# Row-wise dot products with running maximum and record count: one loop for all position groups, and tail masks made in pairs

## Chip, core and metric

The kernel runs on one core of a Trainium2 chip. The metric is the device time of one execution in microseconds; less is better.

## What is computed

```
B, S, D = 8, 2048, 4096            # x: (8, 2048, 4096), w: (4096, 1), float32
proj = (x @ w).squeeze(-1)         # (8, 2048): one dot product of 4096 for each row of x
cm = np.maximum.accumulate(proj, axis=1)
is_record = (proj >= cm).astype(np.float32)
return np.cumsum(is_record, axis=1)
```

For each batch and position: the dot product of a row of x with w, the running maximum over the positions, and a running count of the positions at which the maximum was reached. x is 268 MB and is read once; everything else is small.

## The kernel before

Rows of x lie in the 128 partitions, r of them side by side in each. Work is staged in four groups of positions, `RS = (4, 4, 4, 3)` rows per partition. A tile is one batch of one group: 128 partitions x r x 4096 numbers, 8 MB with four rows and 6 MB with three. Each group has eight tiles, batch 7 first. Then comes a tail: the last 128 positions, as eight tail tiles of 2 MB that hold four batches x 32 positions each, one row per partition; tail tiles 6 and 7 are cut into seven pieces by columns (`LAST`), so that little is left to do after the last one lands.

Three buffers (`xbuf`) hold the tiles. SP issues every load, in program order (L170 for the groups, L198 for the tail), and each load waits until the user before of its buffer is done: `free()` names the semaphore, `fr[t]`, which DVE and ACT each raise once, or `p7` for tile 7, which PE raises. In the first three groups tile t lies in buffer t mod 3, so tiles 6 and 7 lie in buffers 0 and 1, and tiles 0 and 1 of the group after take these again; in the fourth group `at` shifts the buffers by two. Tail tiles 0 to 2 lie in the quarter of the buffers which three-row tiles leave free, the others in the places of tiles 5 and 6.

A row is split by columns. DVE multiplies and sums the first 2816 columns in one instruction per row (`dot`, L126). POOL multiplies the last 1280 columns in place, one instruction per row (`tensor_mul`, L278), and ACT sums the products of each row (`add_up`, L132) as soon as POOL has raised `pl` for it. So each partition ends with two partial sums per row, `sum_v` and `sum_p`.

After a group's last tile PE (`group_rows`, L305 to L319) resets the semaphores and turns the partial sums into rows: two matmuls with the identity per row of the partition, which add `sum_p` and `sum_v` in PSUM (`ps`: 8 batches x 512 positions). DVE then runs `scans` (L140 to L150): running maximum, comparison, running count. Each engine has its own loop over the first three groups (`V.Fori`, `G.Fori`, `A.Fori`, `T.Fori`), and the fourth group's code stands after it in a straight line. DVE's loop begins with the scan of the group before; for the first group that is a scan of a constant (L248).

In the tail (L372 to L414) a tile's sums stand in partitions that mix batches and positions. Two constants sort them: `by_b` (partition to batch) and `by_i` (partition to position). For each tail tile POOL masks DVE's sum with `by_b` (`pick`, L349) and ACT masks its own (`pick_a`, L354); after every second tile PE multiplies the masks with `by_i` (`turn`, L359). DVE's scans of the fourth group stand behind tail tile 2 (384 positions), those of the tail behind tail tile 4 (64), behind piece 1 (32) and at the end (32). In each engine's queue the instructions stand in the order in which this Python code calls them.

Of the kernel before, what the change touches and what calls it, by code (L numbers as in the profile page):

```python
# [13 lines left out]
ALU = mybir.AluOpType  # L14
ACTF = mybir.ActivationFunctionType
NEG = -3.0e38
LOW = -3.2e38
# [3 lines left out]
def kernel(  # L21
# [16 lines left out]
    P = 128  # L38
# [3 lines left out]
    RS = (4, 4, 4, 3)  # L42
    R = RS[0]
    NS = 3
    NG = len(RS)
    NL = NG - 1
    N = R * P
    STARTS = [sum(RS[:g]) * P for g in range(NG)]
    S0 = sum(RS) * P
    assert S0 + P == S  # L50
# [5 lines left out]
    H = 4  # L56
    Q = P // H
# [9 lines left out]
    SEED = (None, 0, None, None, 2, 3, 4)  # L67
# [22 lines left out]
    masked = sb([P, 10 * B], "masked")  # L90
# [13 lines left out]
    sum_v, sum_p = cut(R * B), cut(R * B)  # L104
# [6 lines left out]
    def sem(name):  # L111
# [4 lines left out]
    ws, bw, wc, cs, od, oe, psr, pd, pl, sd, pa, con, fo, ms, p7, mg, pg, ml = (  # L116
        sem(n) for n in "ws bw wc cs od oe psr pd pl sd pa con fo ms p7 mg pg ml".split()
    )

    xq = [(ws, 32), (bw, NW + 16), (wc, 3 + 16), (con, 7 + 16), (fo, 1 + 16)]  # L120
    xq += [(s, 32) for s in xs[:5]] + [(s, 2 * NG + 16) for s in fr[:3]]
# [30 lines left out]
    def at(g, t):  # L152
        return xbuf[(t if g < NL else t + NS - 1) % NS]

    def user_before(g, t):
        if t >= NS:
            return t - NS, g + 1
        if g == NL:
            return B - NS + t, g
        return max(u for u in range(B) if u % NS == t), g  # L160
# [3 lines left out]

    with tc.tile_critical(no_gpsimd_drain=True):

        for g in range(NG):
            r = RS[g]
            for t in range(B):
                i = SY.dma_start(  # L170
                    out=at(g, t)[:, : r * D],
                    in_=x[B - 1 - t, STARTS[g] : STARTS[g] + r * P, :].rearrange(
                        "(p r) d -> p (r d)", r=r
                    ),
                ).then_inc(xs[t], 16)
                u, n = user_before(g, t)
                if n:
                    i._wait_ge(*(free(u, n)))
                if g == t == 0:
                    A.dma_start(  # L180
                        out=w_row, in_=w.rearrange("(k c) one -> k (c one)", k=NW)
                    ).then_inc(ws, 16)
                if t == 4 and g:
                    SY.dma_start(
                        out=out[:, STARTS[g - 1] : STARTS[g]], in_=cnt
                    )._wait_ge(cs, g + 1).then_inc(od, 16)

        def slot(m):
            if m < NS:
                return None, xbuf[m][:, RS[-1] * D :]  # L190
            u = B - NS if m < 2 * NS else B - NS + 1
            return u, at(NL, u)[:, (m % NS) * D : (m % NS + 1) * D]

        freed = {None}
# [23 lines left out]
        G.memset(cm[:, N - 1 :], NEG).then_inc(con, 1)  # L218
        G.memset(cnt[:, N - 1 :], 0.0).then_inc(con, 1)
# [3 lines left out]
        for n, k in enumerate(order):  # L223
# [15 lines left out]

        V.tensor_reduce(  # L240
            out=by_b, in_=identity.rearrange("p (i b) -> p b i", b=H),
            op=ALU.add, axis=mybir.AxisListType.X,
        )._wait_ge(con, 7)
        V.tensor_reduce(  # L244
            out=by_i, in_=identity.rearrange("p (i b) -> p i b", b=H), op=ALU.add,
            axis=mybir.AxisListType.X,
        ).then_inc(fo, 1)
        V.memset(ps[:B, :N], LOW)._wait_ge(wc, 3).then_inc(psr, 1)  # L248

        def group_scans(r=R):  # L250
            n = r * P
            scans(cm[:, :n], cnt[:, :n], ps[:B, :n], cm[:, N - 1 :], cnt[:, N - 1 :])

        def group_dots(r, g=0):
            for t in range(B):
                b, xb = B - 1 - t, at(g, t)
                for j in range(r):
                    i = dot(
                        xb[:, j * D : j * D + VC], w_v[:, :VC],
                        sum_v[:, j * B + b : j * B + b + 1],  # L260
                    )
                    if j == 0:
                        i._wait_ge(xs[t], 16)
                i.then_inc(fr[t], 1)

        with V.Fori(0, NL):
            group_scans()
            V.sem_inc(psr, -3)
            group_dots(R)
        group_scans()  # L270
        V.sem_inc(psr, -3)
        group_dots(RS[-1], NL)

        def group_products(r, g=0):
            for t in range(B):
                for j in range(r):
                    xl = at(g, t)[:, j * D + VC : (j + 1) * D]
                    i = G.tensor_mul(out=xl, in0=xl, in1=w_sb).then_inc(pl, 1)  # L278
                    if j == 0:
                        i._wait_ge(xs[t], 16)  # L280

        G.wait_ge(wc, 3)
        with G.Fori(0, NL):
            group_products(R)
            G.wait_ge(pg, 1).then_inc(pg, -1)
        group_products(RS[-1], NL)

        def group_sums(r, g=0):
            for t in range(B):
                b = B - 1 - t  # L290
                for j in range(r):
                    i = add_up(
                        at(g, t)[:, j * D + VC : (j + 1) * D],
                        sum_p[:, j * B + b : j * B + b + 1],
                    )._wait_ge(pl, j + 1)
                i.then_inc(fr[t], 1)
                A.sem_inc(pl, -r)
            A.wait_ge(pd, 1).then_inc(pd, -1)

        with A.Fori(0, NL):  # L300
            group_sums(R)
        group_sums(RS[-1], NL)

        def group_rows(r):
            T.wait_ge(fr[B - 1], 2).then_inc(p7, 1)  # L305
            T.sem_inc(fr[B - 1], -2)
            if r == R:
                for s in xs:
                    T.sem_inc(s, -16)
                T.sem_inc(pg, 1)  # L310
            T.wait_ge(od, 16).then_inc(od, -16)  # L311
            for j in range(r):
                for k, l in enumerate((sum_p, sum_v)):
                    i = T.matmul(  # L314
                        out=ps[:B, j : r * P : r], lhsT=l[:, j * B : (j + 1) * B],
                        rhs=identity, start=k == 0, stop=k == 1,
                    )
                    if j == r - 1:
                        i.then_inc((pd, psr)[k], 1)  # L319

        with T.Fori(0, NL):
            group_rows(R)
        group_rows(RS[-1])
# [34 lines left out]
        def turn(n, k, start, stop):  # L358
            return T.matmul(  # L359
                out=ps[:B, k * Q : (k + 1) * Q], lhsT=masked[:, n * B : (n + 1) * B],  # L360
                rhs=by_i, start=start, stop=stop,
            )

        def tail_scans(k0, k1, base):
            c = S0 - STARTS[-1]
            a, b = k0 * Q, k1 * Q
            scans(
                cm[:, c + a : c + b], cnt[:, c + a : c + b], ps[:B, a:b],
                cm[:, c + a - 1 : c + a], cnt[:, c + a - 1 : c + a], base,
            )  # L370

        for m in range(B - 2):  # L372
            k = m // 2
            v, p = acc_v[:, m : m + 1], acc_p[:, m : m + 1]
            sums(m, v, p)
            pick_a(col(2 * k, m), p)
            pick(G, col(2 * k + 1, m), v)._wait_ge(sd, nv).then_inc(mg, 1)
            if m == 2:
                group_scans(RS[-1])
            if m == 4:  # L380
                tail_scans(0, 2, 4)
            if m % 2:
                if k != 1:
                    T.wait_ge(cs, NG + 1 + k // 2)
                turn(2 * k, k, True, False)._wait_ge(ms, m + 1)
                mm = turn(2 * k + 1, k, False, True)._wait_ge(mg, m + 1)
                if k:
                    mm.then_inc(psr, 1)

        npart = [0, 0]  # L390
        for i in range(B - 2, len(TILES)):
# [8 lines left out]
            if p:  # L400
                pick_a(col(6 + npart[z], m), dp)
                npart[z] += 1
            if n in (1, len(LAST) - 2):
                pick(G, col(8, m), v)._wait_ge(sd, nv).then_inc(mg, 1)
            if n == 1:
                tail_scans(2, 3, 7)
        assert npart == [2, 2]
        pick(V, col(9, 1), v)._wait_ge(sd, nv).then_inc(ml, 1)
        T.wait_ge(cs, NG + 3)
        turn(6, 3, True, False)._wait_ge(ms, B - 2 + 3)  # L410
        turn(7, 3, False, False)._wait_ge(ms, B - 2 + 4)
        turn(8, 3, False, False)._wait_ge(mg, B)
        turn(9, 3, False, True)._wait_ge(ml, 1).then_inc(psr, 1)
        tail_scans(3, 4, 10)  # L414
        for a, b, n in ((STARTS[-1], S0, 1), (S0, S, 4)):
            SY.dma_start(
                out=out[:, a:b], in_=cnt[:, a - STARTS[-1] : b - STARTS[-1]]
            )._wait_ge(cs, NG + n).then_inc(oe, 16)
# [31 lines left out]
```

## Time and profile before

| | us |
|---|---|
| median of three runs (629.64, 630.08, 630.17) | 630.08 |
| the profiled execution | 629.62 |
| its span, first to last instruction | 627.84 |
| DVE busy | 407.2 |
| POOL busy | 370.5 |
| ACT busy | 181.1 |
| PE busy | 29.4 |

The difference between the profiled execution and its span, 1.78 us, lies around the span. In the lines of the profile, L126 is line 126 of the kernel; "a<-b" is the tile written and those read; "DVE xall L126" in a wait or a chain is what the waiting engine was released by. SPq and PEq are the instruction queues of SP and PE.

The order of one four-row tile in mid-run, from the timeline (start, duration): it lands and POOL starts at 139.52, four products to 151.01; ACT's first sum starts at 142.45 and its last read-out ends at 152.41; SP issues the next load into that buffer at 152.43. The next tile's products start at 158.82, 19.3 us after this one's.

### The profile page before, as it was taken

The numbers are of one execution on the slowest core, as the hardware profiler recorded it, in microseconds if no ns is written. First come the engines' busy times: TensorE is split into PE (matmuls) and PEld (weight loads), VectorE is DVE, ScalarE is ACT, GpSimd is POOL, SyncE is SP. The second block draws the span as 40 slices with busy tenths as digits, with TensorE's granted clock in tenths as the row PEclk, the third lists the DMA queues.
The fourth block names the chain that finished last, engine by engine and source line by source line (L and its number), as shares of the span: only waits on it lengthen the run. The fifth ranks groups of instructions, "written<-read, shape, count | busy, mean of one in ns | idle before, by whom it ended". The sixth has DMA issues, their size and how long they took to land. (4 is left out here: it accounts for less than half of the span.)

```text
span 627.8 us, 1141 instructions
## 1 busy us (share of the span) xinstructions
PE 29.4 (5%) x96; PEld 13.6 (2%) x96; DVE 407.2 (65%) x294; ACT 181.1 (29%) x274; POOL 370.5 (59%) x149
## 2 busy tenths in 40 slices
PE   8000000000020000000001000000002000000110
PEld 3000000000010000000000000000001000000000
DVE  0755676456776557755578655676556976655797
ACT  1222332123322233222233222332223333232244
POOL 0554676456765557745567555676557666655775
PEclk9999999999999999999996555555555555555565
DMA  9999999999999999999999999999999999999996
GB/s 402 401 468 401 468 401 464 406 463 405 463 405 463 405 463 405 465 405 463 405 463 405 463 405 459 409 460 409 459 420 423 436 442 420 443 442 410 430 429 261
DMA packets 6579, 268.55 MB, mean 428 GB/s; under 512 B 768, under 2 KB 1040, under 8 KB 1584
## 3 DMA queue, kind: packets, MB, share of 16 engines
q1 hardware_dynamic: 6560, 268.50, 98.9%
q14 instruction: 3, 0.02, 0.0%
q10 hardware_dynamic: 16, 0.02, 0.0%
HBM read 268.45 MB, written 0.07 MB: 428 GB/s over the span
## 5 line engine op out<-in xcount | busy, mean ns | idle before, releaser
L126 DVE CUSTOM_DVE_ANT_0 xall<-xall,w_v 128x2816 f32<-128x2816 f32 (+1 forms) x129 | 385.5, 3041 | 180.5 <-DMA xall<-in_x_dram 180.5
L278 POOL TENSOR_TENSOR xall<-xall,w_sb 128x1280 f32<-128x1280 f32 x120 | 344.8, 2905 | 245.9 <-DMA xall<-in_x_dram 242.6
L132 ACT ACTIVATE xall<-xall 128x1280 f32<-128x1280 f32 (+2 forms) x130 | 162.9, 1253 | 427.7 <-POOL xall L278 407.2
L314 PE MATMUL ps<-identity,small 128*8 128x128 f32 x60 | 13.4, 415 | 567.2 <-PEq L311 567.2
L132 ACT ACTIVATION_READ_ACCUMULATOR xall<-xall 128x1 f32 x130 | 24.2, 186 | 0.0
L338 POOL TENSOR_TENSOR xall<-xall,w_sb 128x1280 f32<-128x1280 f32 (+2 forms) x8 | 21.0, 2628 | 3.1 <-DMA xall<-in_x_dram 3.0
L314 PEld LDWEIGHTS ps<-identity,small 128*8 128x8 f32 x60 | 7.5, 128 | 574.3 <-issue 570.2
L142 DVE TENSOR_TENSOR_SCAN cm<-ps,cm,small 8x512 f32<-8x512 f32 (+3 forms) x8 | 7.0, 869 | 19.2 <-PE ps L314 18.8
L226 PE MATMUL w_v<-w,identity 8*128 8x512 f32 x14 | 12.2, 1056 | 0.0
L126 DVE DVE_READ_ACCUMULATOR2_ANT small<- 128x1 f32 x133 | 10.8, 81 | 0.0
L248 DVE MEMSET ps<- 8x512 f32 x1 | 0.5, 485 | 15.7 <-ACT w L237 15.7
L148 DVE TENSOR_TENSOR_SCAN cnt<-ps,cnt,small 8x512 f32<-8x512 f32 (+3 forms) x8 | 7.0, 871 | 0.3
L226 PEld LDWEIGHTS w_v<-w,identity 8*128 8x128 f32 x14 | 4.6, 332 | 7.3 <-issue 7.3
L234 ACT COPY w_sb<-w_v 128x768 f32<-128x768 f32 x1 | 0.8, 798 | 11.4 <-PE w_v L226 11.4
L145 DVE TENSOR_TENSOR ps<-ps,cm 8x512 f32<-8x512 f32 (+3 forms) x8 | 3.9, 486 | 0.3
L349 POOL TENSOR_TENSOR masked<-fold,small 128x4 f32<-128x4 f32 x8 | 1.6, 200 | 3.2 <-DVE small L126 3.2
L126 DVE CUSTOM_DVE_ANT_0 xall<-xall,w_v,small 128x480 f32<-128x480 f32 (+2 forms) x4 | 3.1, 810 | 0.2 <-DVE small L126 0.2
L359 PE MATMUL ps<-fold,masked 128*8 128x32 f32 x20 | 2.0, 234 | 25.3 <-ACT masked L354 17.7
L354 ACT ACTIVATE masked<-fold,small 128x4 f32<-128x4 f32 x10 | 3.0, 298 | 0.3
L338 POOL TENSOR_TENSOR xall<-xall,w 128x640 f32<-128x640 f32 (+1 forms) x2 | 2.3, 1136 | 0.1
L226 PE MATMUL ps<-w,identity 8*128 8x512 f32 x2 | 2.1, 1136 | 2.6 <-DMA w<-in_w_dram 2.6
L233 ACT ACT_TABLE_LOAD x1 | 1.3, 1283 | 2.7 <-DVE fold L244 2.7
(18 smaller groups left out, 5.3 us busy)
## 6 DMA issues: line engine op xcount, KB each, us to landing
xall<-in_x_dram SPq DMA_DIRECT2D x8, 6144.0 KB, 33.5
xall<-in_x_dram SPq DMA_DIRECT2D x6, 2048.0 KB, 42.6
xall<-in_x_dram SPq DMA_DIRECT2D x1, 1264.0 KB, 36.6
xall<-in_x_dram SPq DMA_DIRECT2D x1, 816.0 KB, 39.3
xall<-in_x_dram SPq DMA_DIRECT2D x1, 784.0 KB, 37.9
xall<-in_x_dram SPq DMA_DIRECT2D x2, 240.0 KB, 26.6
xall<-in_x_dram SPq DMA_DIRECT2D x1, 416.0 KB, 39.4
xall<-in_x_dram SPq DMA_DIRECT2D x24, 45.0
```

The costliest lines, as they stand in the source:

```text
L126: return V.tensor_tensor_reduce(out=xsl, in0=xsl, in1=wsl, scale=1.0, scalar=seed, op0=ALU.mult, op1=ALU.add, accum_out=dst,)
L132: return A.activation(out=xsl, in_=xsl, func=ACTF.Copy, accum_out=dst)
L142: V.tensor_tensor_scan(out=cm_, data0=src, data1=low, initial=cm0, op0=ALU.max, op1=ALU.max,)._wait_ge(psr, base).then_inc(psr, 1)
L145: V.tensor_tensor(out=src, in0=src, in1=cm_, op=ALU.is_ge)._wait_ge(psr, base + 1).then_inc(psr, 1)
L148: V.tensor_tensor_scan(out=cnt_, data0=src, data1=low, initial=cnt0, op0=ALU.add, op1=ALU.max,)._wait_ge(psr, base + 2).then_inc(cs, 1)
L226: i = T.matmul(out=dst, lhsT=identity[:NW, k : k + 1].to_broadcast([NW, P]), rhs=w_row, start=True, stop=True,).then_inc(bw, 1)
L278: i = G.tensor_mul(out=xl, in0=xl, in1=w_sb).then_inc(pl, 1)
L314: i = T.matmul(out=ps[:B, j : r * P : r], lhsT=l[:, j * B : (j + 1) * B], rhs=identity, start=k == 0, stop=k == 1,)
L338: G.tensor_mul(out=xl, in0=xl, in1=w_pool(*p))._wait_ge(*xq[i]).then_inc(pl, 1)
L349: return eng.tensor_tensor(out=e, in0=by_b, in1=acc.to_broadcast([P, H]), op=ALU.mult)
L354: return A.activation(out=e, in_=by_b, func=ACTF.Copy, scale=acc)._wait_ge(pa, na).then_inc(ms, 1)
L359: return T.matmul(out=ps[:B, k * Q : (k + 1) * Q], lhsT=masked[:, n * B : (n + 1) * B], rhs=by_i, start=start, stop=stop,)
```

## The change

All engines run one loop over four groups (`nc.Fori(0, NG)`). The first three are as before, eight tiles of 128 partitions x 4 rows. The fourth has six tiles of the same 8 MB, each of four batches x 128 positions: a partition holds four positions of one batch. Tiles 6 and 7, PE's matmuls and DVE's scan stand under an `If` that is false in the fourth round; the scan stands now behind the group's tiles. `at` is t mod 3 in all groups. The sixth tile is loaded in two halves, with a semaphore of its own for the second (`xh`).

POOL multiplies the four rows of a tile in one instruction, with w repeated for each; of the sixth tile two rows in each of two instructions. ACT waits once for it and then sums the four rows.

After the loop POOL adds `sum_v` and `sum_p` of the fourth group and masks them all in one instruction each (L355, L359), and PE makes the rows from them in 12 matmuls with `by_i`. In the tail, POOL waits after every second tile for DVE's and ACT's sums of both, adds them and masks them (L425, L429), and PE needs one matmul for a pair. The scan of the fourth group's 384 positions and that of the first 64 of the tail are one scan of 448 behind tail tile 4. Tail tiles 0 to 3 are loaded into the place of tile 3, the others into that of tile 4. The second piece of tail tile 6 no longer starts from the first one's sum; POOL masks both instead. The constants `by_i` are made by POOL. DVE's and ACT's programs are aligned (`addr_align`).

Instructions built: DVE 182 before and 129 now, ACT 117 and 83, POOL 113 and 76, PE 67 and 72, SP 68 and 74.

The diff, cut to what the text speaks of:

```diff
-    RS = (4, 4, 4, 3)
-    R = RS[0]
+    R = 4
     NS = 3
...
-    SEED = (None, 0, None, None, 2, 3, 4)
+    SEED = (None, None, None, None, 2, 3, 4)
...
-    def at(g, t):
-        return xbuf[(t if g < NL else t + NS - 1) % NS]
+    def at(t):
+        return xbuf[t % NS]
...
+                else:
+                    b0, s0 = (1 - t % 2) * H, STARTS[g] + t // 2 * P
+                    src = x[b0 : b0 + H, s0 : s0 + P, :].rearrange(
+                        "b (q r) d -> q b (r d)", r=R
+                    )
...
+                if g == NL and t == NT - 1:
+                    i = SY.dma_start(
+                        out=at(t)[:, :half], in_=src[:, :, :half]
+                    ).then_inc(xs[t], 16)
+                    SY.dma_start(
+                        out=at(t)[:, half:], in_=src[:, :, half:]
+                    ).then_inc(xh, 16)
...
         def slot(m):
-            if m < NS:
-                return None, xbuf[m][:, RS[-1] * D :]
-            u = B - NS if m < 2 * NS else B - NS + 1
-            return u, at(NL, u)[:, (m % NS) * D : (m % NS + 1) * D]
+            u = NT - NS + m // 4
+            return u, at(u)[:, m % 4 * D : (m % 4 + 1) * D]
...
-                for j in range(r):
-                    xl = at(g, t)[:, j * D + VC : (j + 1) * D]
-                    i = G.tensor_mul(out=xl, in0=xl, in1=w_sb).then_inc(pl, 1)
...
+        def products(t):
+            rows = at(t).rearrange("p (r d) -> p r d", r=R)
+            n = R // 2 if t == NT - 1 else R
+            for j in range(0, R, n):
+                xl = rows[:, j : j + n, VC:]
+                i = G.tensor_mul(
+                    out=xl, in0=xl, in1=w_one.to_broadcast([P, n, PC])
+                ).then_inc(pl, 1)
+                landed(i, t, j)
...
+        def row_sums(t):
+            for j in range(R):
+                c = COL(t, j)
+                i = add_up(at(t)[:, j * D + VC : (j + 1) * D], sum_p[:, c : c + 1])
+                if j == 0 or t == NT - 1 and j == R // 2:
+                    i._wait_ge(pl, 1)
...
+        with nc.Fori(0, NG) as g:
+            for t in range(NT):
+                dots(t)
+                products(t)
+                row_sums(t)
+            with nc.If(NL - g):
+                for t in range(NT, B):
+                    dots(t)
+                    products(t)
+                    row_sums(t)
+                G.wait_ge(pg, 1).then_inc(pg, -1)
+                A.wait_ge(pd, 1).then_inc(pd, -1)
+                group_rows()
+                scan_to(0, N, 1)
+                V.sem_inc(psr, -3)
...
         for m in range(B - 2):
             k = m // 2
             v, p = acc_v[:, m : m + 1], acc_p[:, m : m + 1]
             sums(m, v, p)
-            pick_a(col(2 * k, m), p)
-            pick(G, col(2 * k + 1, m), v)._wait_ge(sd, nv).then_inc(mg, 1)
-            if m == 2:
-                group_scans(RS[-1])
             if m == 4:
-                tail_scans(0, 2, 4)
+                scan_to(0, NE + 2 * Q, 1)
             if m % 2:
-                if k != 1:
-                    T.wait_ge(cs, NG + 1 + k // 2)
-                turn(2 * k, k, True, False)._wait_ge(ms, m + 1)
-                mm = turn(2 * k + 1, k, False, True)._wait_ge(mg, m + 1)
+                two = sum_t[:, 2 * k : 2 * k + 2]
+                G.wait_ge(sd, nv)
+                G.tensor_tensor(
+                    out=two, in0=acc_v[:, m - 1 : m + 1], in1=acc_p[:, m - 1 : m + 1],
+                    op=ALU.add,
+                )._wait_ge(pa, na).then_inc(mk, 1)
+                G.tensor_tensor(
+                    out=masked[:, k * B : (k + 1) * B].rearrange("p (z b) -> p z b", b=H),
+                    in0=two.rearrange("p (z o) -> p z o", o=1).to_broadcast([P, 2, H]),
+                    in1=by_b.rearrange("p (o b) -> p o b", o=1).to_broadcast([P, 2, H]),
+                    op=ALU.mult,
+                )._wait_ge(mk, 3 + k).then_inc(mg, 1)
+                if k == 2:
+                    T.wait_ge(cs, NL + 1)
+                mm = turn(k, k, True, True)._wait_ge(mg, k + 1)
...
-            if n in (1, len(LAST) - 2):
-                pick(G, col(8, m), v)._wait_ge(sd, nv).then_inc(mg, 1)
+            if n in (0, 1, len(LAST) - 2):
+                pick(G, col(5 + (n == 0), m), v)._wait_ge(sd, nv).then_inc(mg, 1)
             if n == 1:
-                tail_scans(2, 3, 7)
+                scan_to(NE + 2 * Q, NE + 3 * Q, 4)
```

## Prediction

> **What bounds the kernel now.** I read the page's head first, then the time slices, the queues, the waits of the DMA queue, and last the order of time at the end of the run.
>
> ```profile
> span 627.8 us, 1141 instructions
> DMA  9999999999999999999999999999999999999996
> q1 hardware_dynamic: 6560, 268.50, 98.9%
> ```
> The load queue holds all 16 DMA engines for 98.9% of the span: the stream of x is the bound, in every slice but the last.
>
> ```profile
> SPq L170 <- ACT xall L132: 414.2, 20, 38.9
> ```
> SP waits 414 us in all for ACT to free a buffer, yet the DMA engines never run dry: each load is issued while at least one whole tile is still moving. That wait is cover, and I ask below where it gets thin.
>
> ```profile
> 480.00:500.00 20.00, 3.57 (x16) 1.97 (x16) 13.66 (x12) 5.04 (x9) 11.59 (x5) 0.50 1.01 435
> 622.00:623.00 1.00, 0.00 (x0) 0.00 (x0) 1.00 (x5) 0.97 (x3) 0.73 (x1) 0.50 0.13 47
> 623.00:624.00 1.00, 0.28 (x3) 0.11 (x4) 1.00 (x4) 0.90 (x4) 0.20 (x1) 0.50 0.00 0
> ```
> (Last column GB/s.) 435 GB/s in mid-run; the last byte starts before 623. From there to the end, 627.84, nothing but the tail is left: about 4.9 us.
>
> ```profile
> 613.21 3.09 DVE L126 CUSTOM_DVE_ANT_0 xall<-xall,w_v 128x2816 f32<-128x2816 f32 x1 [0.89 <-DMA xall<-in_x_dram]
> 613.26 2.90 POOL L338 TENSOR_TENSOR xall<-xall,w_sb 128x1280 f32<-128x1280 f32 x1 [1.53 <-DMA xall<-in_x_dram]
> ...
> 616.39 0.20 POOL L349 TENSOR_TENSOR masked<-fold,small 128x4 f32<-128x4 f32 x1 [0.23 <-DVE small L126]
> 616.54 1.88 POOL L338 TENSOR_TENSOR xall<-xall,w_sb 128x800 f32<-128x800 f32 x1
> ...
> 620.19 1.75 POOL L338 TENSOR_TENSOR xall<-xall,w_sb 128x736 f32<-128x736 f32 x1
> ```
> Start, duration, and in brackets the idle time before. At tail tile 5 (613.2) both engines still waited for data, by 0.89 and 1.53 us: that is all the slack left there. After it they run almost back to back.
>
> ```profile
> 620.19 1.76 POOL xall L338
> 621.95 0.02 issue
> 621.97 0.92 ACT xall L132 x2
> 622.88 0.02 issue
> 622.91 0.30 ACT masked L354
> 623.21 0.41 ACT xall L132 x2
> 623.61 0.02 issue
> 623.64 0.31 ACT masked L354
> ```
> The chain that ended last: POOL's product of 736 columns, ACT's sum, mask, sum, mask (to 623.95), then PE and the last scans to 625.41, output to 627.84. DVE's own last mask ends at 624.24, so both end within 0.3 us of each other.
>
> [...] here 1280 elements take 2.90 us and 256 take 0.73, a slope of 2.12 ns plus 0.19 fixed[...]. [...] The trace shows three instruction packets, 0.0%, and no idle time of DVE, ACT or POOL put down to fetching, so shorter programs have nothing visible to win. [...]
>
> ```profile
> POOL masked L349 <- DVE small L126: 3.2, 5, 1.4
> ```
> POOL idles up to 1.4 us for a mask with its next product queued behind.
>
> **The change, part by part.** All in the profiled execution's frame (span 627.84, run 629.62); it lies 0.46 below the median, and I add the sum to the median.
>
> *Loads.* The same 268 MB. Packets of 64 KiB take 2.418 us and of 48 KiB 1.815 (the trace's packet records); per DMA engine 64 x 1.815 = 116.16 becomes 48 x 2.418 = 116.06: -0.1 us. The four-batch pattern is the tail's own (L198), which already moves 423 GB/s and more with rows of 16 KiB; I take no change. Tail landings thus move by -0.1.
>
> *One product of four rows, then four sums.* Before, a tile was free about 12.9 us after landing: tile 6 of the first group landed at 139.5 and SP issued the next load into its buffer at 152.43. Now POOL's 5120 elements take 0.19 + 5120 x 2.12 = 11.0 us (by slope) to 11.5 (four rows as now), and only then ACT sums four rows, each 1.27 + 0.19 overlapped to about 1.38: 5.5. Sum 16.6 to 17.1. Within a group three buffers rotate, and 19.3 us more cover it. At a group's end they do not: tiles 6 and 7 use buffers 0 and 1, and tiles 0 and 1 of the next group want these two again. Cover there is one tile: landing to the dry queue is 19.32 - 0.43 (last packet to landing) = 18.9 us for the slowest DMA engine and 18.3 for the others (the packet records show one 0.6 us behind); from issue to first packet takes 1.03 (0.97 to 2.00 at the start). 17.1 + 1.0 = 18.1. So it still fits, by 0.2 to 0.8 us. Cost taken: 0, three times. Without the cover, it costs 3 x the overrun.
>
> *Start.* DVE loses a memset and an empty first scan (18.29 to 22.11), POOL gains two small additions at 2 us; both end before the first tile lands (22.8). 0.
>
> *Scan at the loop's end.* DVE waits for PE there and then starts tile 0: about 5 + 3.2 us late, under a tile period of 19.3 against 12.3 of work; SP's output DMA waits behind tile 1's buffer anyway. 0. The same for branches, the nine semaphore steps on PE, and SP's empty loop, which runs after its last load is issued (about 603.6) and before its last store (625.4).
>
> *Last tile in halves, and its masks.* Its second half lands at about 583.9; POOL ends it at 589.7, ACT at 592.6. POOL waits for that (L355), then two small operations (0.45 together, from the 0.20 mask rows, bounds 0.3 to 0.8): first tail product at 593.35 against 592.69. The wait for data absorbs this: before tile 5 POOL is through at 611.9 by the same sum, and that tile lands at 613.1.
>
> *Pairs on POOL in the tail.* Removed: six ACT masks and six POOL masks. Added: after every second tile POOL waits for ACT's sum of the tile it has just multiplied, then adds, then masks. For tile 5: landing 613.1, product to 616.05, ACT (1.27 + 0.19 with its start) to 617.45, add and mask to 617.95. Before, POOL went on at 616.54. Behind it in its queue stand the products of the last two tiles: 800 columns 618.0 to 619.9, mask 0.2 (an added one), 640 columns to 621.7, mask to 621.9, 736 columns to 623.7. Before, that last one ended at 621.95. From there ACT's chain is unchanged, 2.0 us (621.95 to 623.95): 625.7. Three short matmuls wait for it, 0.5, then the scans from 626.25 against 624.61: **+1.65 us**. Price range: add and mask 0.3 to 0.8, so +1.5 to +2.0; if ACT's sum were somehow early, the DVE path below is left.
>
> *One scan of 448 in place of 384 and 64.* It stands after tile 4, no longer after 2. By size (384: 2.56 us, 64: 0.96) 448 takes 2.9. DVE: tile 4 to 611.3, scan to 614.2, tile 5 1.0 us late; then back to back 3.0, 1.88, 1.11, 0.72 (scan), 1.0, 0.94, 0.57, 0.64, 0.71, mask: 625.0 against 624.24: +0.75, beside POOL's path and under it.
>
> Sum +1.65: 631.3 in the profile's frame, **631.7** as median.
>
> **Rivals.** (a) Forecast, POOL's pair wait sets the end: 631.7. For it: the 1.53 us of slack is less than what is added. (b) POOL's small operations or ACT are quicker than taken and DVE's scan sets the end: 630.08 + 0.75 = 630.8; against it, 0.9 us would have to vanish. (c) Not slower: the shorter programs save around the span. Its place is the 1.78 us between run and span (629.62 - 627.84) and the 0.97 before the first load; a saving of 1.65 gives 630.1, and from 0.4 on the change can no longer be told from none. DVE goes from 182 to 129 instructions, ACT 117 to 83, POOL 113 to 76; against it stand the three packets[...]. (d) The two buffers at the group's end are late: if the four-row product with its repeated w takes 12.5 instead of 11.5, or the first packet comes later, 3 x 0.8 on top: 634. It decides from about 11.8 us per product. For it: the margin is the thinnest in the run. (e) Products in rows are far slower on POOL, past 19.3 us a tile: POOL becomes the bound, 30 x 23 = 690.
>
> **Chances.** (a) 0.62, (b) 0.14, (c) 0.08, (d) 0.14, (e) 0.02. A difference of 0.2%, 1.26 us, is about what measuring this kernel tells from none; that line is at 631.34. Slower by more: most of (a) (0.54), (d), (e): 0.70. Within: the rest of (a), (b), most of (c): 0.28. Faster: 0.02, as the stream alone ends at 622.9. Range 630.4 to 633.4: (a), (b) and the near part of (d), leaving out (c), the far part of (d) and (e).
>
> **What would show it.** POOL's first product of the last two tiles starts near 618 with no DMA wait before it; L425 shows about 1.4 us waits for ACT, three times; the chain that ends last goes POOL, ACT, PE, DVE, ending near 629.5. DMA 9 in all slices: a bubble at 157, 312 and 467 us, or a landing gap over 19.4, would be (d). Last x bytes at 622.8. I am wrong if the tail's POOL reaches the 736 product before 621, or the stream ends after 623.5.

## Result and profile after

| | before | changed |
|---|---|---|
| median, us (five runs each) | 629.78 | 636.84 |
| lowest to highest | 629.64 to 630.17 | 636.08 to 636.97 |
| span of the profiled execution | 627.8 | 634.7 |

The ratio is 1.0107, 95% interval [1.0092, 1.0121]: slower by 7.1 us, where 1.6 was forecast. The time lies above the stated range (630.4 to 633.4).

From the head of the changed kernel's page, and its load queue:

```profile
span 634.7 us, 1139 instructions
...
DMA  9999999999999999999999999999999999999994
...
q1 hardware_dynamic: 6416, 268.50, 98.4%
```

The row of nines says that nothing happened. A nine is any share of 90% or more in 15.9 us: a gap of 1 us is invisible there, and 98.4% instead of 98.9% is 3 us of all 16 engines in a longer span. The gap has to be looked for where the forecast's rival (d) put it, at the group ends. First POOL's order of time around the third of them (start, duration, in brackets the idle time before), for tiles 6 and 7 and tile 0 of the next group, in the changed kernel:

```profile
451.44 11.05 POOL L302 TENSOR_TENSOR xall<-xall,w_sb 128x5120 f32<-128x5120 f32 x1 [8.13 <-DMA xall<-in_x_dram]
470.76 11.04 POOL L302 TENSOR_TENSOR xall<-xall,w_sb 128x5120 f32<-128x5120 f32 x1 [8.26 <-DMA xall<-in_x_dram]
492.42 11.02 POOL L302 TENSOR_TENSOR xall<-xall,w_sb 128x5120 f32<-128x5120 f32 x1 [10.62 <-DMA xall<-in_x_dram]
```

POOL starts 0.07 us after a landing, so its starts show the landings: 19.32 us from tile 6 to 7, but 21.66 to tile 0. In the kernel before, tile 0 follows tile 7 by 19.32 us, as evenly as any other (the first group end):

```profile
158.82 11.49 POOL L278 TENSOR_TENSOR xall<-xall,w_sb 128x1280 f32<-128x1280 f32 x4 [7.81 <-DMA xall<-in_x_dram]
178.14 11.49 POOL L278 TENSOR_TENSOR xall<-xall,w_sb 128x1280 f32<-128x1280 f32 x4 [7.83 <-DMA xall<-in_x_dram]
```

At the changed kernel's third group end SP issues tile 0's load, into the buffer of tile 6, at 467.67:

```profile
467.67 0.63 SPq L194 DMA_DIRECT2D xall<-in_x_dram  x1
```

It comes 16.3 us after tile 6 landed and 3.0 us before tile 7 landed. The DMA engines around it (last two columns: busy share, GB/s by the start of packets):

```profile
466.00:468.00 2.00, 0.00 (x0) 0.00 (x0) 0.00 (x0) 1.65 (x4) 0.00 (x0) 0.50 0.76 328
468.00:469.00 1.00, 0.00 (x0) 0.00 (x0) 0.00 (x0) 0.00 (x0) 0.00 (x0) 0.50 0.01 0
469.00:470.00 1.00, 0.00 (x0) 0.00 (x0) 0.00 (x0) 0.00 (x0) 0.00 (x0) 0.50 3.07 983
```

Packets last 2.42 us and are counted where they start, so single columns swing. But two us at 328, one at 0 and one at 983 make 410 GB/s on average, where the kernel before moved 435 in mid-run, and by the packet records three packets are moving just before 469.07: 13 of the 16 engines are empty at once. Fifteen engines start their next packet 1.40 to 1.95 us after SP's issue. The sixteenth has data until 470.36 and starts its next packet at 471.69, 4.02 us after the issue. These first packets take 2.8 to 3.7 us instead of 2.42; at the kernel's start 14 of the 16 take 2.9 to 3.5. The tile's last packet ends on the sixteenth engine, at 492.00, and POOL starts at 492.42. That engine loses 1.33 us empty and 0.94 us in a packet of 3.36: nearly all of the 2.34 by which tile 0 is late.

"Slip" below is how much later tiles 0 and 1 landed together than two periods of 19.32 after tile 7. At the three group ends it is 0.85, 1.42 and 2.33 us: 4.6.

The end, in the chain that ended last:

```profile
618.36 2.91 POOL xall L390
621.30 1.37 ACT xall L134 x2
622.67 0.07 issue
622.74 0.20 POOL small L425
622.94 0.07 issue
623.01 0.20 POOL masked L429
623.21 1.83 POOL xall L390
625.04 0.16 POOL masked L401
625.21 1.49 POOL xall L390
626.70 0.16 POOL masked L401
626.86 1.71 POOL xall L390
628.59 0.92 ACT xall L134 x2
...
631.66 0.27 DVE cnt L150
```

The chain of the kernel before ended with:

```profile
625.14 0.27 DVE cnt L148
```

This is the forecast's tail, line by line: tail tile 5, ACT's sum, POOL's two small operations, then the products of the last two tiles with no wait for data before them. From the start of POOL's product of tail tile 5 to the end of the last scan it takes 13.57 us (618.36 to 631.93), before 12.15 (613.26 to 625.41): +1.42.

So of 6.9 us of span, tail tile 5 comes 5.1 late (618.36 against 613.26: 4.6 at the group ends, 0.26 at the first landing, 0.2 elsewhere), the tail adds 1.4, and the end after the last scan 0.3. The executions also spend more time around the span: 2.2 us instead of 1.8 (636.97 against a span of 634.7, 629.62 against 627.8). No run here shows what it is.

### The profile page after: what moved, and what is told of

Its sections match the earlier page's. It is cut to its first block, busy times and chain, and to the rows that moved or that the text cites. A ratio compares the mean times of both kernels' runs of the same rounds, so it can differ in the third digit from the quotient of the medians.

```text
span 634.7 us, 1139 instructions
## 1 busy us (share of the span) xinstructions
PE 27.5 (4%) x102; PEld 13.2 (2%) x102; DVE 402.8 (63%) x286; ACT 169.8 (27%) x268; POOL 358.7 (57%) x68
## 3 DMA queue, kind: packets, MB, share of 16 engines
q1 hardware_dynamic: 6416, 268.50, 98.4%
## 4 chain that ended last, share of the span: by engine, by line
DMA 69%; POOL 21%; ACT 7%; issue 2%; SPq 0%; DVE 0%; PE 0%; PEldq 0%
DMA xall<-in_x_dram 69%; POOL xall L302 19%; ACT xall L134 7%; POOL xall L390 1%; ACT masked L406 0%; SPq L216 0%; PE ps L411 0%; SPq L194 0%; POOL masked L401 0%; DVE cm L144 0%; DVE cnt L150 0%; POOL small L425 0%; POOL masked L429 0%; DVE ps L147 0%; PEldq L320 0%
## 5 line engine op out<-in xcount | busy, mean ns | idle before, releaser
L128 DVE CUSTOM_DVE_ANT_0 xall<-xall,w_v 128x2816 f32<-128x2816 f32 (+2 forms) x130 | 386.6, 3026 | 196.0 <-DMA xall<-in_x_dram 172.3
L302 POOL TENSOR_TENSOR xall<-xall,w_sb 128x5120 f32<-128x5120 f32 (+1 forms) x34 | 331.8, 9764 | 260.3 <-DMA xall<-in_x_dram 236.2
L328 PE MATMUL ps<-identity,small 128*8 128x128 f32 x48 | 10.5, 411 | 456.9 <-PEq L325 456.9
L144 DVE TENSOR_TENSOR_SCAN cm<-ps,cm,small 8x512 f32<-8x512 f32 (+2 forms) x6 | 5.5, 914 | 30.0 <-PE ps L328 28.9
L328 PEld LDWEIGHTS ps<-identity,small 128*8 128x8 f32 x48 | 6.1, 130 | 462.4 <-issue 459.2
L370 PE MATMUL ps<-fold,gmask 128*8 128x32 f32 x24 | 1.4, 241 | 105.8 <-POOL gmask L359 105.8
L150 DVE TENSOR_TENSOR_SCAN cnt<-ps,cnt,small 8x512 f32<-8x512 f32 (+2 forms) x6 | 5.5, 915 | 0.2
L370 PEld LDWEIGHTS ps<-fold,gmask 128*8 128x8 f32 x24 | 1.3, 115 | 106.3 <-POOL gmask L359 106.3
L147 DVE TENSOR_TENSOR ps<-ps,cm 8x512 f32<-8x512 f32 (+2 forms) x6 | 3.1, 510 | 0.2
L425 POOL TENSOR_TENSOR small<-small 128x2 f32<-128x2 f32 x3 | 0.6, 194 | 4.4 <-ACT xall L134 4.4
```

The costliest lines, as they stand in the source:

```text
L128: return V.tensor_tensor_reduce(out=xsl, in0=xsl, in1=wsl, scale=1.0, scalar=seed, op0=ALU.mult, op1=ALU.add, accum_out=dst,)
L144: V.tensor_tensor_scan(out=cm_, data0=src, data1=low, initial=cm0, op0=ALU.max, op1=ALU.max,)._wait_ge(psr, base).then_inc(psr, 1)
L147: V.tensor_tensor(out=src, in0=src, in1=cm_, op=ALU.is_ge)._wait_ge(psr, base + 1).then_inc(psr, 1)
L150: V.tensor_tensor_scan(out=cnt_, data0=src, data1=low, initial=cnt0, op0=ALU.add, op1=ALU.max,)._wait_ge(psr, base + 2).then_inc(cs, 1)
L302: i = G.tensor_mul(out=xl, in0=xl, in1=w_one.to_broadcast([P, n, PC])).then_inc(pl, 1)
L328: i = T.matmul(out=ps[:B, j:N:R], lhsT=l[:, j * B : (j + 1) * B], rhs=identity, start=k == 0, stop=k == 1,)
```

## Experiments

"Group end" below is the landing of tiles 6 and 7 and of tiles 0 and 1 after them; "ahead" is the time from SP's issue of a load to the landing of the tile before it in the queue. Kernels measured together share the runs of the kernel before (629.77 and 629.83). Times are medians; figures of group ends are from the profiled execution.

**rows67: the two boundary tiles row by row.**

```diff
+        def SPLIT(t):
+            return (1,) * 4 if t >= NT else (2, 2) if t == NT - 1 else (4,)
...
-            n = R // 2 if t == NT - 1 else R
-            for j in range(0, R, n):
+            j = 0
+            for n in SPLIT(t):
...
-                if j == 0 or t == NT - 1 and j == R // 2:
+                if j in firsts:
                     i._wait_ge(pl, 1)
```

`NT` is 6, and `firsts` holds the first row of each piece: ACT waits for each piece of POOL's work.

> Tiles 6 and 7 alone get their products row by row again, as before the change; everything else stays. Theory 1 (the two buffers that are taken again at once at a group's end come free about 3.4 us later than before, and the load queue runs dry at the three group ends): both tiles free about 12.9 us after landing, no gap there, 4.7 us back: about 631.9. Theory 2 (the shared loop, its branches and its If, or the fetching of instructions, disturbs the loads): stays within 0.5 of 636.8. Theory 3 (loads of four batches by 128 positions are slower): most of the third group end's 2.3 us stays: about 634.3.

Measured: 631.35 (630.99 to 631.92), ratio 1.0025 [1.0013, 1.0036]. 5.5 us are back by touching two of eight tiles. The third group end, POOL first, then SP:

```profile
467.95 11.51 POOL L305 TENSOR_TENSOR xall<-xall,w_sb 128x1280 f32<-128x1280 f32 x4 [7.80 <-DMA xall<-in_x_dram]
487.27 11.03 POOL L305 TENSOR_TENSOR xall<-xall,w_sb 128x5120 f32<-128x5120 f32 x1 [7.81 <-DMA xall<-in_x_dram]
```

```profile
461.57 0.62 SPq L194 DMA_DIRECT2D xall<-in_x_dram  x1
```

The load is issued 6.3 us before tile 7 lands, and the landings are 19.32 apart again. The loop, its branches and its If are all still there, and the load is one of four batches x 128 positions: both other theories fall.

**rows05: the mirror.** Row by row in tiles 0 to 5, one product in tiles 6 and 7 (`SPLIT` returns `(1,) * 4 if t < NT else (4,)`).

> The mirror of the run before: products row by row in tiles 0 to 5, one product of four rows in tiles 6 and 7. Theory 1: only tiles 6 and 7 matter, so nothing comes back: 636.0 to 637.0. A theory that the long product or the run of four sums hurts in every tile: most of the loss comes back, about 632.

Measured: 635.94 (635.74 to 636.59). Group ends cost 0.99, 1.25 and 1.76. 0.9 of the 7.1 us come back, and the group ends still cost 4.0: in the tiles inside a group the long product is covered, as forecast.

**before_late: the kernel before, with late issues.**

```diff
+                if 0 < g < NL and t < 2:
+                    SY.wait_ge(*free(u, n))
+                    for _ in range(20):
+                        SY.sem_inc(dl, 1)
+                        SY.sem_inc(dl, -1)
                 i = SY.dma_start(
```

> The kernel before, with one thing added: at the first two group ends SP spends 40 semaphore steps between the freeing of a buffer and the issue of tile 0's and tile 1's load (2 to 4 us). The computation and the order of the data are unchanged. Theory 1: if the issue comes as late as in the changed kernel (155.5 instead of 152.4 at the first group end), the landing of tile 0 slips by 0.3 to 1.5 us at each of the two: 630.5 to 632.5. If a late issue is harmless and something else in the change cost the time: 629.8.

Measured: 631.29 (629.98 to 632.48, 14 runs), ratio 1.0025 [1.0016, 1.0033]. The first group end, POOL's starts, then SP's issues of tile 1 and 2:

```profile
159.27 11.49 POOL L285 TENSOR_TENSOR xall<-xall,w_sb 128x1280 f32<-128x1280 f32 x4 [7.79 <-DMA xall<-in_x_dram]
178.56 11.49 POOL L285 TENSOR_TENSOR xall<-xall,w_sb 128x1280 f32<-128x1280 f32 x4 [7.80 <-DMA xall<-in_x_dram]
198.85 2.90 POOL L285 TENSOR_TENSOR xall<-xall,w_sb 128x1280 f32<-128x1280 f32 x1 [8.80 <-DMA xall<-in_x_dram]
```

```profile
175.11 0.80 SPq L177 DMA_DIRECT2D xall<-in_x_dram  x2
```

With the added steps tile 0's load is issued 15.4 us after tile 6 landed, 2.4 later than without them (13.0). Tile 0, issued 3.9 us ahead, lands on time (19.29); tile 1, issued 3.4 us ahead (175.11 to 178.5), lands 1.0 late (20.29). At the second group end both are issued 3.9 to 4.1 us ahead, and neither slips. So the time is within the expected range, but the place is not: tile 1 was late instead of tile 0, at one group end of two. The 14 runs spread over 2.5 us, those of the kernel before over 0.6. A late issue alone, in a kernel without any of the change, makes a loss of the same kind.

**late: the changed kernel, later still.** The same steps on SP, 20 of them, at all three group ends.

> The changed kernel, with 20 semaphore steps on SP (about 1.5 us by the run of the kernel before with 40) between the freeing of the buffer and the issue of tile 0's and tile 1's loads at all three group ends. Theory 1: the load queue is dry at once and for longer, each group end costs 1.2 to 2 us more: 640 to 643. If the group ends' cost does not hang on the issue: 636.8.

Measured: 639.47 (637.94 to 640.44), a little under the expected range. Tile 0 is issued 17.5 to 18.0 us after tile 6 landed, 1.3 to 2.0 ahead; the group ends cost 2.98, 2.23 and 3.27. DMA at the third one:

```profile
470.00:480.00 10.00, 0.00 (x0) 0.00 (x0) 7.19 (x5) 0.00 (x0) 7.14 (x1) 0.50 0.81 315
471.00:472.00 1.00, 0.00 (x0) 0.00 (x0) 0.00 (x0) 0.00 (x0) 0.00 (x0) 0.50 0.01 0
```

Now even a window of 10 us shows it: 81% busy, 315 GB/s.

**one_three: between the two.** Tiles 6 and 7 in products of one row and of three (`SPLIT` returns `(1, 3)` for them).

> The changed kernel with the products of tiles 6 and 7 cut into one row and three rows, so that ACT sums one row early and the buffers come free about 1.3 us sooner than now (15.0 instead of 16.3 after landing, 12.9 in the kernel before). Theory 1 says that this is where the edge lies: between 631.4 (no gap left) and 633.5 (a gap at some group ends, as at one of four in the kernel before with late issues at 15.4).

Measured: 632.18 (631.99 to 633.44), ratio 1.0043 [1.0028, 1.0059]. In its profile tile 0 is issued 15.2 us after tile 6 landed, 4.1 ahead, and no group end slips. The median stands 0.8 above rows67, and all four runs are above its seven. The two profiles put most of that difference at the end: tail tile 5 (613.22 and 613.17) and the tail (13.55 and 13.57 us) agree, but from the last scan to the end of the span it is 2.9 us instead of 2.5. Why is not shown.

What the group ends say together. The trace has 16 landing marks for each load, the steps of its semaphore; taken as one from each DMA engine, the first and the last show how far the engines are apart. The three middle columns are those of tile 0's load, group end by group end.

| kernel | issue after tile 6 landed | ahead of the last mark of tile 7 | ahead of its first mark | slip of tiles 0 and 1 |
|---|---|---|---|---|
| before (two ends) | 13.0 | 6.3 | 5.2, 5.3 | 0, 0 |
| rows67 | 13.0 | 6.5, 6.4, 6.3 | 6.2, 6.1, 6.0 | 0.08, 0, 0 |
| one_three | 15.2 | 4.2, 4.2, 4.1 | 3.8, 3.9, 3.8 | 0, 0, 0 |
| before_late (two ends) | 15.4, 15.3 | 3.9, 4.1 | 3.0, 2.4 | 0.95, 0 |
| changed | 16.3 | 3.0, 3.1, 3.0 | 2.6, 1.6, 0.9 | 0.85, 1.42, 2.33 |
| rows05 | 16.3 | 3.1, 3.1, 3.0 | 2.3, 1.4, 1.5 | 0.99, 1.25, 1.76 |
| masks_old (below) | 16.3 | 3.1, 3.0, 3.2 | 2.4, 1.3, 1.0 | 0.94, 1.57, 0.23 |
| late | 17.5, 18.0, 17.5 | 1.8, 1.3, 2.0 | 1.2, -1.0, 0.7 | 2.98, 2.23, 3.27 |

The fourth column tells why the slips grow in the changed kernel although the issue is equally late each time. In its trace an engine that has fallen behind stays behind: tile 7's marks are 0.47 us apart at the first group end, 1.46 at the second and 2.08 at the third, and hardly change in between (1.30 for tile 1 after the first group end, 2.02 after the second). So the engines that lead have ever less left to move when the issue comes. The 0.23 of masks_old is the exception that fits: there the leading engines lose too (the first mark slips by 1.6 in sum), but the last engine goes on without a gap at 470.11, so its landing hardly moves and the spread closes from 2.20 to 0.81.

**masks_old: the tail's pair masks undone, group ends left.**

> The tail's pair masks are undone: ACT and POOL each mask their own sum after every tail tile again, PE adds two masks per tile; the one scan of 448 positions stays. If POOL's wait for ACT in the tail is worth what the forecast said, 0.8 to 1.0 us come back (the scan of 448 then sets the end, 0.75 above the old): about 635.9. If the tail's wait is hidden, 636.8.

Measured: 634.94 (634.02 to 636.29). 1.9 come back, but as much as that can be its luckier group ends (2.74 in sum against 4.6), which differ from run to run. The time alone says nothing of the tail; in the trace the tail takes 13.06 us (616.11 to 629.17) instead of 13.57. The next two take the group ends away first.

**rows67_masks and all_undone: the tail, step by step.** The edits, shortened:

```diff
# rows67_masks, on top of rows67
-                G.wait_ge(sd, nv)
-                G.tensor_tensor(out=two, ..., op=ALU.add)._wait_ge(pa, na)
-                G.tensor_tensor(out=masked[...], ..., op=ALU.mult)
-                mm = turn(k, k, True, True)._wait_ge(mg, k + 1)
+            pick_a(col(2 * k, m), p)
+            pick(G, col(2 * k + 1, m), v)._wait_ge(sd, nv).then_inc(mg, 1)
+                turn(2 * k, k, True, False)._wait_ge(ms, m + 1)
+                mm = turn(2 * k + 1, k, False, True)._wait_ge(mg, m + 1)
# all_undone, on top of rows67_masks
+            if m == 2:
+                scan_to(0, NE, 1)
             if m == 4:
-                scan_to(0, NE + 2 * Q, 1)
+                scan_to(NE, NE + 2 * Q, 4)
```

> Tiles 6 and 7 row by row, and the tail's pair masks undone as well (each engine masks its own sum after every tail tile); the single scan of 448 stays. With the group ends out of the way (that alone measured 631.35), this shows what POOL's wait for ACT in the tail costs. Forecast's tail: the pair wait sets the end by 1.65 and DVE's single scan would by 0.75, so 0.8 to 0.9 come back: 630.5. If only the pair wait cost and the scan nothing: 629.8.

Measured: 630.84 (630.67 to 631.34), ratio 1.0016 [1.0009, 1.0023]: the pair masks are worth 0.5 on top of the scan (631.35 - 630.84). Its chain now runs through DVE's scan of 448:

```profile
607.95 3.09 DVE xall L128
611.04 1.06 DVE cm L144
612.13 0.63 DVE ps L147
612.78 1.14 DVE cnt L150
613.92 2.98 DVE xall L128
```

> As the run before, and the scan of 448 is cut again into 384 behind tail tile 2 and 64 behind tail tile 4. What is left of the change: one loop, the If, the fourth group's six tiles of four batches, one product of four rows in tiles 0 to 4. Theory: nothing that sets the end is left, 629.7, within 0.3 of the kernel before. If the loop or the four-batch tiles cost something of their own: above 630.3.

Measured: 629.87 (629.44 to 630.29, 13 runs), ratio 1.0001 [0.9993, 1.0009]: the scan was worth 1.0, and nothing is left. One loop on all engines, the If, six tiles of four batches, and one product of four rows in tiles 0 to 4 cost nothing, to within the interval of about 0.5 us. They gain nothing either, as the stream of x still sets the time (POOL's starts at the third group end, 467.85 and 487.17, show landings 19.32 us apart); no version among these beats the kernel before.

## Why the prediction was wrong, step by step

**The step that failed** is "So it still fits, by 0.2 to 0.8 us. Cost taken: 0, three times." The tile was free even earlier than taken: 16.3 us after landing, not 16.6 to 17.1 (POOL's product took 11.04; four sums of ACT, 5.1). What was mis-sized is the other side, the time that a load needs to take over. The prediction took 1.03 us from issue to first packet. That is the fastest engine at the kernel's start, where the 16 take 1.03 to 1.56. In the changed kernel, at the first group end, one engine starts its first packet of tile 1 only 3.02 us after the issue, after some 0.7 us empty; at the third, one starts its first packet of tile 0 4.02 us after it. Nor did the sum have a term for the slow packet after a gap, or for the spread of the engines growing beyond the 0.6 us of the kernel before.

By the prediction's sum the edge lay at 17.3 to 17.9 us after landing, 1.4 to 2 us ahead. Measured, nine loads issued 3.9 to 4.2 us ahead (one_three, before_late) did not slip; one at 3.4 slipped by 1.0; nine of tile 0 at 3.0 to 3.2 by 0 to 2.3; three below 2.1 by 2.3 to 3.3. The prediction's reading of SP's waits, "each load is issued while at least one whole tile is still moving", was wrong already for the kernel before: at a group end only the last 6.3 us of tile 7 were left, a third of a tile.

The size was wrong as well. The prediction priced the loss as the overrun times three. Measured it is rather a step: 1.3 to 2.0 ahead, where an overrun of up to 0.7 was to be expected, costs 2.2 to 3.3 at each group end. Rival (d) named the place and, beside a longer product, the cause: "or the first packet comes later". It got 0.14; its trigger for the product ("from about 11.8 us") was not met, as the product took 11.0, and its 634 priced the group ends at 2.4 us where they cost 4.6.

**The tail was right in its mechanism.** Forecast was +1.65, and in the traces of the changed kernel and of rows67 the tail is +1.42. That the times of rows67 and of its runs of before differ by nearly the forecast, 631.35 - 629.77 = +1.58, is in part luck: only 1.0 of it lies in the spans (medians 629.0 and 628.0), and 0.6 around them (2.4 us instead of 1.8), which the forecast held to be unchanged. POOL's first product of the last two tiles was forecast 4.9 us after tail tile 5's landing and started at 4.87; three waits of "about 1.4 us" for ACT were 1.47 each:

```profile
POOL small L425 <- ACT xall L134: 4.4, 3, 1.5
```

Its division was a little off: the scan of 448 alone costs 1.0 (630.84 - 629.87; 0.91 in the trace of rows67_masks), not 0.75, and the pair masks 0.5 more, not 0.9.

**The rest.** Loads of four batches x 128 positions at full rate: right (rows67, 19.32 us per tile). Branches, the shared loop, the later scan, 0: right (all_undone). Shorter programs save nothing, as was said against rival (c): nothing was gained around the span, where the changed kernel spends 0.4 us more. One product of four rows: 11.04 by the slope, at the low end of the forecast's 11.0 to 11.5. The sign of a bubble to look for, a landing gap over 19.4, was right and settled it; so was the sign of being wrong, a stream that ends after 623.5: it ended at 628.6.

**Open.** Why a single engine starts its packet so late, 4.02 us after the issue at the third group end, where the other fifteen take 1.40 to 1.95: the packet records show that it does, without a cause in them. What the longer time around the span is, and why the end after the last scan takes 2.4 to 2.9 us.

## To carry to other kernels

A wait that is all cover still has an edge: for each buffer, compare the time from landing to the next issue with the time until the queue is empty, at the place in the loop where a buffer is taken again soonest (here every eighth tile), not on average. Leave several microseconds there (here some 4), not the 1.03 us from issue to first packet at the start, and measure the margin from the engine that runs empty first; where an operation is merged to save instructions on an engine that has time to spare, see when its consumers start (here the one product of four rows moved the next load's issue from 13.0 to 16.3 us after landing), and split it again just at that place. In a tail that ends soon after its data (here 623.2 to 625.4 in the kernel before), count each wait that has further work queued behind it on its engine (here three of 1.47 us on POOL): that sum held here to about 0.2 us in the trace.

## What was not expected of the hardware

A load that is issued into a queue about to run empty needed a lead of about 4 us here (at 3.9 to 4.2 none of nine slipped, at 3.4 one slipped by 1.0), against 1.03 us from issue to first packet at the kernel's start.

A load of 16 KB (w) from ACT's queue, issued in the changed kernel at 1.35 us instead of 0.92, and so after SP's first load (0.97) instead of before it, landed at 11.0 instead of 2.6, and DVE could start only at 26.8 instead of 22.8:

```profile
26.82 3.09 DVE L128 CUSTOM_DVE_ANT_0 xall<-xall,w_v 128x2816 f32<-128x2816 f32 x1 [23.74 <-ACT w L255]
```

It cost nothing here: SP issues the next load into tile 0's buffer at 43.02 instead of 35.79, and what it loads lands at 80.97, 19.30 us after the tile before. That the order of the two issues is the cause is read from the two traces; no run changes it alone. 0.4 us on the other queue went with 8.4.
